# Chaining the chunk products of a state-space scan in TensorE's queue, in six of eight groups

## The chip, the cores and the metric

The kernel runs on one core of one Trainium2 chip. The metric is device time in microseconds of one execution. Three executions of the kernel before were timed, and one more was run under the hardware profiler.

## What is computed

One layer of a hybrid sequence model on a 1024 x 1024 input: a normalised and modulated input `u` goes through one wide projection `w_in`, which feeds a short convolution branch and a Mamba-2 scan; both are projected back, merged by gates, projected by `w_o`, and followed by a squared-ReLU MLP and a last normalisation. The change lies in the scan, which the reference writes so:

```
def step(state, inp):
    xq, aq, bq, cq = inp
    a_cum = jnp.cumsum(aq, axis=1)
    ...
    scores = jnp.einsum('btgn,bsgn->btsg', cq, bq)
    y_diag = jnp.einsum('btsg,btsgr,bsgrp->btgrp', scores, decay, xq)
    y_off = jnp.einsum('btgn,bgrpn->btgrp', cq, state) * jnp.exp(a_cum)[..., None]
    ...
    new_state = (state * jnp.exp(a_cum[:, -1])[..., None, None]
                 + jnp.einsum('bsgn,bsgr,bsgrp->bgrpn', bq, to_end, xq))
    return new_state, y_diag + y_off
```

There are 32 heads in 8 groups; the four heads of a group share `b` and `c`. The kernel cuts the 1024 positions into 8 chunks of 128, which gives the same result as the reference's 16 chunks of 64. All values are float32.

## The kernel before

**Stages.** The projections of the gates, of `z` and of the short convolution come first and last to about 634 us. From there to about 1240 us the scan runs, one group after another (`ssd_group`, L772), and beside it the projections that feed the later groups (`proj_group`, L746). After it come the branch projections (`wco`, L908, begins beside groups 5 to 7; `wso`, from L937), the output projection and the MLP, to 2102 us.

**One chunk of one group** needs five kinds of products on TensorE. The text uses these names for them:

- the *scores* (L779 to L782): the product of `b` and `c` and three transposes, into the PSUM tile `A`, of which there are two;
- the *inner outputs* (L802): four small products of the masked and decayed scores `seg` with `xd`, into the first half of the one PSUM tile `B`;
- the *state outputs* (L807): two products of `c` with the running state, into the second half of `B`; chunk 0 has none;
- the *state update* (L824): one product of `bt` and `xe`, into the one PSUM tile `C`; chunk 7 has none;
- and, once in each group from the second on, the *row sums* of the group before (`finish`, L847; L858 and L859, two pairs), which use the same PSUM tile `C`, after the state update of chunk 4 and before that of chunk 5.

Between them VectorE makes `smk`, `xd`, `xe` out of the scores, multiplies `seg` by `smk`, adds the two outputs (`t1`, L814 and L815), writes them into `xs` (L821, which frees `B`), and forms the next state (L830, L831). ScalarE makes the exponentials out of `acb`, which a transfer on SP's queue brings (L777), and copies `bt`. The tiles of the pool `p2` exist twice.

**The projections beside it.** `proj_group(g + 1)` is traced after the scan of group `g`. It makes four tiles (`xbc_tile`, L732): two of `xs`, one of `bf`, one of `cf`; each is 48 matmuls of 128 x 512 (L121, L122 and L124, 16 each), then two copies by ScalarE into one of two `raw` buffers, a four-tap convolution (ScalarE, three VectorE operations of 1024 columns into one of two `cacc` buffers), and an activation whose result goes to `xs`, `bf` or `cf` of the pool `p2g[g % 2]`. Group `g + 2` writes the same buffers as group `g`, so that this last step waits until the scan of group `g` has read them for the last time.

**What sets the order.** Nobody writes the order of the queues here. A planner in the framework orders each engine's instructions when the kernel is built, by modelled times; what is queued on an engine is then fixed. `tc.issue_after(ins)` adds edges for that planner: what the block traces on the engine of `ins` stands behind `ins` in that engine's queue. It is an edge of order alone; nothing waits for `ins` to end. The kernel before uses it in this stage for the row sums only (L857: behind the state update of chunk 4, which `last` holds).

Of the kernel before, what the change touches and what calls it, by code (L numbers as in the profile page):

```python
# [16 lines left out]
P = 128  # L17
# [21 lines left out]
def hybrid_trunk(tc, xT, par, hrows, crow, wada1, wadak, wada2, win, wdt, wco, wso, wo, wup, wdt_, wdn, out):  # L39
    nc = tc.nc  # L40
    pe, act, dve, pool, sp = nc.tensor, nc.scalar, nc.vector, nc.gpsimd, nc.sync

    def tt(o, a, b, op, eng=dve):
        return eng.tensor_tensor(out=o, in0=a, in1=b, op=op)  # L44

    def stt(o, a, s, b, op0, op1):
        return dve.scalar_tensor_tensor(out=o, in0=a, scalar=s, in1=b, op0=op0, op1=op1)  # L47
# [13 lines left out]
    ident = cp.tile([P, P], F32, name="ident")  # L61
# [471 lines left out]
    for k in range(4):  # L533
# [3 lines left out]
        for i, t in enumerate(ts4):  # L537
            o = [tks[-1].tile([P, H], F32R, name=f"t{i}{j}") for j in (0, 1)]
# [233 lines left out]
    def ssd_group(g, xs, bf, cf, prev):  # L772
        state = None
        for c in range(NC_):
            cs = slice(c * P, c * P + P)
            acb = p2.tile([P, 4, P], F32, name="acb")
            sp.dma_start(acb, ac_d[4 * g:4 * g + 4, cs].partition_broadcast(P))  # L777
            A = psA.tile([P, 512], F32, name="A")
            pe.matmul(A[:, 0:P], lhsT=bf[:, cs], rhs=cf[:, cs], start=True, stop=True)  # L779
            pe.transpose(A[:, 128:256], xs[:, 0, cs], ident)  # L780
            pe.transpose(A[:, 256:384], xs[:, 1, cs], ident)
            pe.transpose(A[:, 384:512], bf[:, cs], ident)  # L782
            smk = p2.tile([P, P], F32, name="smk")
            tt(smk, A[:, 0:P], tri, ALU.mult)
            xd = p2.tile([P, 4, 64], F32, name="xd")
            xq = A[:, 128:384].rearrange("p (r k) -> p r k", r=4)
            tt(xd, xq, dt_t[:, c, 4 * g:4 * g + 4].unsqueeze(2).broadcast_to([P, 4, 64]), ALU.mult)
            if c < NC_ - 1:
                bt = p2.tile([P, P], F32, name="bt")
                act.copy(bt, A[:, 384:512])  # L790
                xe = p2.tile([P, 4, 64], F32, name="xe")
                tt(xe, xq, de_t[:, c, 4 * g:4 * g + 4].unsqueeze(2).broadcast_to([P, 4, 64]), ALU.mult)
            seg = p2.tile([P, 4, P], F32, name="seg")
            for r in range(4):
                hd = 4 * g + r
                act.activation(seg[:, r, :], acb[:, r, :], AF.Relu, bias=acum[:, c, hd:hd + 1], scale=-1.0)
            act.activation(seg, seg, AF.Exp, scale=-1.0)
            tt(seg, seg, smk.unsqueeze(1).broadcast_to([P, 4, P]), ALU.mult)
            Bk = psB.tile([P, 512], F32, name="B")
            for r in range(4):  # L800
                o = 64 * (r % 2)
                pe.matmul(Bk[o:o + 64, P * (r // 2):P * (r // 2) + P], lhsT=xd[:, r, :], rhs=seg[:, r, :],  # L802
                          start=True, stop=True, skip_group_check=True)
            ydv = Bk[:, 0:256].rearrange("p (q t) -> p q t", q=2)
            if c > 0:
                for q in (0, 1):
                    pe.matmul(Bk[:, 256 + P * q:256 + P * q + P],  # L807
                              lhsT=state[:, 2 * q:2 * q + 2, :].rearrange("p r k -> p (r k)"),
                              rhs=cf[:, cs], start=True, stop=True, skip_group_check=True)
                ebc = p2.tile([P, 2, P], F32, name="ebc")  # L810
                for q in (0, 1):
                    act.activation(ebc[64 * q:64 * q + 64], acb[64 * q:64 * q + 64, q::2, :], AF.Exp)
                t1 = p2.tile([P, 2, P], F32, name="t1")
                tt(t1, Bk[:, 256:512].rearrange("p (q t) -> p q t", q=2), ebc, ALU.mult)  # L814
                tt(t1, ydv, t1, ALU.add)  # L815
                src = t1
            else:
                src = ydv
            for q in (0, 1):
                col = DSK + 2 * g + q  # L820
                stt(xs[:, q, cs], xs[:, q, cs], prm[:, col:col + 1], src[:, q, :], ALU.mult, ALU.add)  # L821
            if c < NC_ - 1:
                C = psC.tile([P, H], F32, name="C")[:, 0:256]
                last = pe.matmul(C, lhsT=bt, rhs=xe.rearrange("p r k -> p (r k)"), start=True, stop=True)  # L824
                ns = p2.tile([P, 4, 64], F32, name="state")
                cv = C.rearrange("p (r k) -> p r k", r=4)
                if c == 0:
                    dve.tensor_copy(ns, cv)
                else:
                    tt(ns, state, edec[:, c, 4 * g:4 * g + 4].unsqueeze(2).broadcast_to([P, 4, 64]), ALU.mult)  # L830
                    tt(ns, cv, ns, ALU.add)  # L831
                state = ns
            if c == 4 and prev is not None:
                finish(prev, last)
            if c == 5:
                zs = [p2.tile([P, T], F32, name="zs") for _ in (0, 1)]
                for q in (0, 1):
                    sp.dma_start(zs[q], z_d[2 * g + q])
            if c == 6 and g in (5, 7):
                rstd(*{5: (0, 4), 7: (4, 6)}[g])  # L840
            yield
        for q in (0, 1):
            tt(zs[q], xs[:, q, :], zs[q], ALU.mult)
            pool.dma_start(y_d[2 * g + q], zs[q])
        return g, zs

    def finish(prev, last):  # L847
        g, zs = prev
        for q in (0, 1):
            act.activation(zs[q], zs[q], AF.Square)  # L850
        tt(zs[0], zs[0], zs[1], ALU.add)
        for h in (0, 1):
            sqh, sql = [p2.tile([P, H], F32R, name=n, bufs=1) for n in ("sqh", "sql")]
            split(sqh, sql, zs[0][:, hs[h]])
            row = p2.tile([1, H], F32, name="row", bufs=1)
            ps = psC.tile([P, H], F32, name="C")
            with tc.issue_after(last.ins):  # L857
                pe.matmul(ps, lhsT=onec, rhs=sqh, start=True, stop=False)  # L858
                pe.matmul(ps, lhsT=onec, rhs=sql, start=False, stop=True)  # L859
            act.copy(row, ps[0:1, :])  # L860
            act.dma_start(ssq_d[g:g + 1, hs[h]], row)

    def rstd(g0, g1):
        n = 8 * (g1 - g0)
        sq = p2.tile([32, P], F32, name="sq", bufs=1)[:n]
        sp.dma_start(sq, ssq_d[g0:g1].rearrange("g (c t) -> (g c) t", t=P))
        r = rsqrt_eps(p2, sq, 1.0 / 1024.0, [n, P], "y")
        tsc(r, r, 0.5, None, ALU.mult, ALU.bypass)
        act.dma_start(rst_d[g0:g1].rearrange("g (c t) -> (g c) t", t=P), r)
# [10 lines left out]
    for g in range(NG - 1):  # L880
        gen = ssd_group(g, *cur, prev)
        prev = None
        while prev is None:
            prev = drive(gen)
        cur = proj_group(g + 1)
# [14 lines left out]
    p2t.release()  # L900
    gp = tc.alloc_tile_pool(name="gp", bufs=3, side="right", reuse_waits="tile")
    gen = ssd_group(NG - 1, *cur, prev)
    prev = None
    for f in range(8):
# [107 lines left out]
    for h in (0, 1):  # L1012
        for i in range(4):
            ps, = proj(ws[i], u2h, u2l, halves=(h,))
            r = p6.tile([P, H], F32, name="hid0", bufs=3)
# [6 lines left out]
    for k in range(4):  # L1022
        for i, t in enumerate(tops_of(x1[k] + x1[k + 4], mcol[:, 28 + k:29 + k], dcs[:, k:k + 1])):
            o = [(sl.tile([P, H], F32R, name="s1") if i == 3 else tp.tile([P, H], F32R, name=f"t{i}{k}{j}")) for j in (0, 1)]
# [87 lines left out]
    for s in range(3):  # L1112
# [26 lines left out]
        for n, blk in enumerate((0, 2, 5, 4, 3, 1, 6)):  # L1139
            t = operand([lambda q=q: stage(op_d[s, 2 * q:2 * q + 2, :, blk, :].rearrange("k p t -> p k t")) for q in (0, 1)])  # L1140
            first = n in (0, 2, 3, 5)
            for q in (0, 1):
# [10 lines left out]
                for i in (0, 1):  # L1153
                    p = 2 * q + i
                    if first:
                        bank[p] = mm.tile([P, H], F32, name="mm")
                    o = bank[p]
                    for k in range(4):
                        c_ = slice(i * H + k * P, i * H + k * P + P)
                        for j, (l_, r_) in enumerate(((wh, 0), (wh, 1), (wl, 0))):  # L1160
                            pe.matmul(o, lhsT=l_[:, c_], rhs=t[:, r_, k, :], start=first and k == j == 0,  # L1161
                                      stop=k == 3 and j == 2, skip_group_check=True)
# [13 lines left out]
    for t0, tw, onpool in PARTS:  # L1176
        h, o = t0 // H, t0 % H
# [90 lines left out]
```

## Time and profile before

| | us |
|---|---|
| median of three timed executions | 2101.52 (2098.99 to 2104.03) |
| the profiled execution | 2104.39 |
| its span, first to last instruction | 2102.6 |
| TensorE busy in the span | 2067.2 |
| VectorE busy | 1491.5 |
| ScalarE busy | 962.1 |
| 680 to 1010 us (scan of groups 0 to 4): TensorE, VectorE, ScalarE busy, of 330 | 330.0, 248.2, 224.4 |

A matmul's recorded time overlaps that of the next one, so that TensorE can be "busy" throughout and still lose a tenth of a microsecond between two starts; for that the text goes by the distance of the starts. The mean TensorE clock of the execution was 0.993 of full speed.

### The profile page before, as it was taken

The page shows a single profiled execution, that of the slowest core. Times are in us where ns is not written, and L with a number is a line of the kernel's source. Part 1 is how long each engine was busy: PE and PEld are TensorE (multiplying, and loading weights), DVE is VectorE, ACT ScalarE, POOL GpSimd, SP SyncE. Part 2 cuts the span into 40 slices and gives each one's busy share as a digit, 9 for nine tenths or more (in the row PEclk, how much of TensorE's full clock was granted, in tenths as well). Part 3 has the DMA queues.
Part 4 walks back from the last instruction along what each step waited for, and adds up shares of the span by engine and source line. Part 5 has one row for each costly group of instructions (what it writes and reads, how often), then busy time and mean ns, then how long its engine had stood idle before and what let it go on. Part 6 is the DMA issues. An engine that isn't in the chain of part 4 may idle for free.

```text
span 2102.6 us, 26286 instructions
## 1 busy us (share of the span) xinstructions
PE 2067.2 (98%) x9736; PEld 1693.4 (81%) x9736; DVE 1491.5 (71%) x2348; ACT 962.1 (46%) x1570; POOL 178.2 (8%) x247
## 2 busy tenths in 40 slices
PE   8999999999999999999999999999999999999997
PEld 6878878888887878887788787888888888888887
DVE  8777876776863777777977867936866665658675
ACT  4433333333335676666754541334544454544432
POOL 0010000000001000000000000012000001232213
PEclk8999999999999999999999999999999999999998
DMA  9345543222228454555365779643144447998932
GB/s 326 107 160 184 184 166 121 96 74 71 81 83 252 108 144 128 145 130 127 117 204 205 258 266 338 230 142 115 60 165 165 157 163 261 302 241 253 277 78 81
DMA packets 142578, 355.65 MB, mean 169 GB/s; under 512 B 13505, under 2 KB 48705, under 8 KB 140914
## 3 DMA queue, kind: packets, MB, share of 16 engines
q1 hardware_dynamic: 100002, 206.43, 30.2%
q0 software_dynamic: 27280, 105.39, 17.4%
q10 hardware_dynamic: 15168, 42.15, 5.1%
q8 instruction: 77, 1.26, 0.2%
q14 instruction: 51, 0.42, 0.1%
HBM read 275.08 MB, written 78.84 MB: 168 GB/s over the span
## 4 chain that ended last, share of the span: by engine, by line
PE 75%; issue 14%; DMA 6%; DVE 3%; ACT 1%; POOL 1%; SPq 0%; DVEq 0%; POOLq 0%; ACTq 0%
PE mm L155 30%; PE mm L1161 9%; PE mm L121 9%; PE mm L124 9%; PE mm L122 9%; PE mm L402 2%; PE B L802 1%; PE B L807 1%; DMA wraw<-in_win 1%; DMA wv<-in_wada 1%; DMA dr<-in_wdt_ 1%; PE C L824 1%; POOL wv L550 1%; DMA acb<-ac_d 1%; PE st L402 1%
## 5 line engine op out<-in xcount | busy, mean ns | idle before, releaser
L155 PE MATMUL mm<-t,whi 128*128 128x512 f32 x1168 | 359.3, 389 | 3.8 <-DVE cq L44 3.8
L155 PEld LDWEIGHTS mm<-t,whi 128*128 128x128 f32 x1168 | 218.8, 188 | 50.8 <-DVE cq L44 5.7
L155 PE MATMUL mm<-t,wlo 128*128 128x512 f32 x584 | 226.6, 389 | 0.0
L1161 PE MATMUL mm<-op,whi 128*128 128x512 f32 x672 | 207.1, 389 | 1.2 <-DVE y L47 0.7
L121 PE MATMUL mm<-uh,whi 128*128 128x512 f32 x448 | 177.7, 397 | 1.4 <-ACT raw L738 1.4
L122 PE MATMUL mm<-ul,whi 128*128 128x512 f32 x448 | 177.4, 396 | 0.0
L44 DVE TENSOR_TENSOR wlo<-s,whi 128x1024 fp32r<-128x1024 f32 (+1 forms) x128 | 129.0, 1019 | 67.4 <-ACT whi L160 66.5
L44 DVE TENSOR_TENSOR wlo<-wraw,whi 128x1024 fp32r<-128x1024 f32 (+1 forms) x136 | 144.8, 1065 | 11.7 <-ACT whi L160 5.4
L121 PE MATMUL mm<-ys,whi 128*128 128x512 f32 x384 | 149.3, 393 | 1.5 <-DVE s L44 1.5
L122 PE MATMUL mm<-ys,whi 128*128 128x512 f32 x384 | 150.0, 392 | 0.0
L1161 PEld LDWEIGHTS mm<-op,whi 128*128 128x128 f32 x672 | 126.0, 188 | 28.2 <-ACT whi L1147 2.0
L124 PE MATMUL mm<-uh,wlo 128*128 128x512 f32 x448 | 142.8, 395 | 0.0
L160 ACT CAST whi<-wraw 128x1024 fp32r<-128x1024 f32 x80 | 66.9, 837 | 161.5 <-PE mm L155 143.4
L155 PE MATMUL mm<-s,whi 128*128 128x512 f32 x448 | 138.0, 389 | 0.7 <-ACT cu L178 0.7
L1161 PE MATMUL mm<-op,wlo 128*128 128x512 f32 x336 | 130.7, 389 | 0.0
L160 ACT CAST whi<-s 128x1024 fp32r<-128x1024 f32 x80 | 84.1, 1052 | 99.2 <-PE mm L155 93.1
L155 PEld LDWEIGHTS mm<-t,wlo 128*128 128x128 f32 x584 | 109.6, 188 | 22.9
L124 PE MATMUL mm<-ys,wlo 128*128 128x512 f32 x384 | 125.8, 392 | 0.0
L155 PE MATMUL mm<-uh,whi 128*128 128x512 f32 x312 | 122.4, 392 | 2.4 <-ACT cu L178 2.4
L47 DVE SCALAR_TENSOR_TENSOR y<-mm,mcol,y 128x512 f32<-128x512 f32 (+1 forms) x100 | 69.3, 704 | 76.1 <-PE mm L1161 40.2
L47 DVE SCALAR_TENSOR_TENSOR cacc<-raw,hw,cacc 128x1024 f32<-128x1024 f32 x84 | 107.1, 1278 | 21.3 <-ACT cacc L740 21.0
L155 PE MATMUL mm<-ul,whi 128*128 128x512 f32 x312 | 121.9, 391 | 0.0
(318 smaller groups left out, 4483.0 us busy)
## 6 DMA issues: line engine op xcount, KB each, us to landing
wraw<-in_win SPq DMA_DIRECT2D x83, 512.0 KB, 3.9
dr<-in_wdt_ SPq DMA_DIRECT2D x108, 256.0 KB, 5.2
op_d<-hp POOLq DMA_DIRECT2D x12, 1792.0 KB, 7.1
hr<-op_d POOLq DMA_DIRECT2D x42, 512.0 KB, 6.0
wv<-in_wada POOLq DMA_DIRECT2D x32, 512.0 KB, 4.3
acb<-ac_d SPq DMA_DIRECT2D x64, 256.0 KB, 6.1
wraw<-in_wup SPq DMA_DIRECT2D x32, 512.0 KB, 4.0
wlo<-in_win POOLq DMA_DIRECT2D x28, 512.0 KB, 7.7
```

The lines of the kernel that those rows point to most:

```text
L44: return eng.tensor_tensor(out=o, in0=a, in1=b, op=op)
L47: return dve.scalar_tensor_tensor(out=o, in0=a, scalar=s, in1=b, op0=op0, op1=op1)
L121: pe.matmul(o, lhsT=wh, rhs=h_, start=start, stop=False)
L122: pe.matmul(o, lhsT=wh, rhs=l_, start=False, stop=False)
L124: last_mm[0] = pe.matmul(o, lhsT=wl, rhs=h_, start=False, stop=stop)
L155: last_mm[0] = pe.matmul(o, lhsT=l_[:, s_], rhs=r_, start=first and k == j == 0, stop=k == 3 and j == 2, skip_group_check=True)
L160: act.copy(hi, src)
L402: pe.matmul(sps[f, h], lhsT=w_[f][:, j * P:j * P + P], rhs=v_[j][h], start=j == i == 0, stop=j == KT - 1 and i == 2, skip_group_check=True)
L550: pool.dma_start(w_, wada2[i])
L802: pe.matmul(Bk[o:o + 64, P * (r // 2):P * (r // 2) + P], lhsT=xd[:, r, :], rhs=seg[:, r, :], start=True, stop=True, skip_group_check=True)
L807: pe.matmul(Bk[:, 256 + P * q:256 + P * q + P], lhsT=state[:, 2 * q:2 * q + 2, :].rearrange("p r k -> p (r k)"), rhs=cf[:, cs], start=True ...
L1161: pe.matmul(o, lhsT=l_[:, c_], rhs=t[:, r_, k, :], start=first and k == j == 0, stop=k == 3 and j == 2, skip_group_check=True)
```

## The change

Two blocks are put behind `last`, and `last` is now set by more products. In groups 0 to 5, the state update of a chunk stands behind the last output product of that chunk (the state outputs, or the inner outputs in chunk 0); the scores of chunks 1 to 7 stand behind the state update of the chunk before. The scores of chunk 0, and all of groups 6 and 7, stay free. No arithmetic, no buffer and no transfer is changed. In the call of `finish`, `last` is still the state update of chunk 4.

```
@@ ssd_group @@
             A = psA.tile([P, 512], F32, name="A")
-            pe.matmul(A[:, 0:P], lhsT=bf[:, cs], rhs=cf[:, cs], start=True, stop=True)
-            pe.transpose(A[:, 128:256], xs[:, 0, cs], ident)
-            pe.transpose(A[:, 256:384], xs[:, 1, cs], ident)
-            pe.transpose(A[:, 384:512], bf[:, cs], ident)
+            with tc.issue_after(last.ins) if c and g < 6 else contextlib.nullcontext():
+                pe.matmul(A[:, 0:P], lhsT=bf[:, cs], rhs=cf[:, cs], start=True, stop=True)
+                pe.transpose(A[:, 128:256], xs[:, 0, cs], ident)
+                pe.transpose(A[:, 256:384], xs[:, 1, cs], ident)
+                pe.transpose(A[:, 384:512], bf[:, cs], ident)
...
             for r in range(4):
                 o = 64 * (r % 2)
-                pe.matmul(Bk[o:o + 64, P * (r // 2):P * (r // 2) + P], lhsT=xd[:, r, :], rhs=seg[:, r, :],
-                          start=True, stop=True, skip_group_check=True)
+                last = pe.matmul(Bk[o:o + 64, P * (r // 2):P * (r // 2) + P], lhsT=xd[:, r, :], rhs=seg[:, r, :],
+                                 start=True, stop=True, skip_group_check=True)
...
                 for q in (0, 1):
-                    pe.matmul(Bk[:, 256 + P * q:256 + P * q + P],
-                              lhsT=state[:, 2 * q:2 * q + 2, :].rearrange("p r k -> p (r k)"),
-                              rhs=cf[:, cs], start=True, stop=True, skip_group_check=True)
+                    last = pe.matmul(Bk[:, 256 + P * q:256 + P * q + P],
+                                     lhsT=state[:, 2 * q:2 * q + 2, :].rearrange("p r k -> p (r k)"),
+                                     rhs=cf[:, cs], start=True, stop=True, skip_group_check=True)
...
                 C = psC.tile([P, H], F32, name="C")[:, 0:256]
-                last = pe.matmul(C, lhsT=bt, rhs=xe.rearrange("p r k -> p (r k)"), start=True, stop=True)
+                with tc.issue_after(last.ins) if g < 6 else contextlib.nullcontext():
+                    last = pe.matmul(C, lhsT=bt, rhs=xe.rearrange("p r k -> p (r k)"), start=True, stop=True)
```

## The prediction, made before the change was run

> **What bounds the kernel now.** I read the page first, then the busy time by stretch, then TensorE's waits, and last the order of time on TensorE in the scan.
>
> ```profile
> PE 2067.2 (98%) x9736; PEld 1693.4 (81%) x9736; DVE 1491.5 (71%) x2348; ACT 962.1 (46%) x1570; POOL 178.2 (8%) x247
> ```
>
> ```profile
> 134.00:140.00 6.00, 3.66 (x9) 2.94 (x10) 5.80 (x11) 3.58 (x7) 0.00 (x0) 0.72 0.07 10
> 680.00:1010.00 330.00, 330.00 (x1787) 265.32 (x1786) 248.18 (x484) 224.42 (x454) 24.35 (x32) 1.00 0.52 129
> 1010.00:1210.00 200.00, 196.44 (x1043) 158.41 (x1042) 164.43 (x294) 116.39 (x229) 2.13 (x4) 1.00 0.61 203
> ```
>
> ```profile
> PE C L824 <- DVE xe L44: 2.0, 2, 1.3
> PE mm L121 <- DVE s L44: 1.5, 1, 1.5
> PE mm L121 <- ACT raw L738: 1.4, 1, 1.4
> PE B L802 <- DVE seg L44: 1.1, 1, 1.1
> PE B L802 <- DVE t L44: 0.8, 1, 0.8
> ```
>
> The columns of the second fence are the stretch and its length, the busy time (and count) of TensorE, weight load, VectorE, ScalarE and GpSimd, the granted clock, the share of the DMA engines and GB/s. In the scan of groups 0 to 4 TensorE is never free, at full clock. The third fence holds all its waits from 660 to 1290 us: 6.8 us together. So this stage ends when TensorE's work ends, and that work is the same after the change: nothing is removed. A gain can come only from cheaper switching between the products, or out of those 6.8 us. A loss has no such cap.
>
> **Switching.** The planner already puts many products side by side. One such run on TensorE (start, duration):
>
> ```profile
> 705.00 0.39 PE L121 MATMUL mm<-uh,whi 128*128 128x512 f32 x1
> 705.32 0.66 PE L802 MATMUL B<-seg,xd 128*64 128x128 f32 x8
> 705.91 0.71 PE L807 MATMUL B<-cf,state 128*128 128x128 f32 x4
> 706.46 0.60 PE L824 MATMUL C<-xe,bt 128*128 128x256 f32 x2
> 706.89 0.38 PE L779 MATMUL A<-cf,bf 128*128 128x128 f32 x2
> ...
> 707.36 0.48 PE L122 MATMUL mm<-ul,whi 128*128 128x512 f32 x1
> 707.67 0.40 PE L121 MATMUL mm<-uh,whi 128*128 128x512 f32 x1
> 707.90 0.39 PE L122 MATMUL mm<-ul,whi 128*128 128x512 f32 x1
> ```
>
> ```profile
> 694.34 0.59 PE L824 MATMUL C<-xe,bt 128*128 128x256 f32 x2
> 694.59 0.59 PE L122 MATMUL mm<-ul,whi 128*128 128x512 f32 x1
> 695.01 0.40 PE L121 MATMUL mm<-uh,whi 128*128 128x512 f32 x1
> ```
>
> A projection product takes 0.23 us of the queue (707.67 to 707.90). From the projection product ahead of the run to the second one behind it are 2.67 us; less two products that leaves 2.2 us for all of a chunk's products. Inside, the state update takes 706.46 to 706.89, 0.43 us. Alone between projection products it takes 694.34 to 695.01 less one product, 0.44 us. So leaving the projections and coming back costs 0.01 us. The change can save one or two such switches in 48 chunks: 0 to 1 us. I take 0.5 us.
>
> **What the edges move.** Before, the state update stands one chunk ahead of its outputs, and the scores up to three. The first fence below is the tile `C` from 970 to 992 us (group 4: count, shortest, median and longest in ns, first and last start), the second is TensorE in order of time:
>
> ```profile
> L824 PE MATMUL C<-xe,bt x4: 377/378/483, 971.4 to 991.8; 128*128 128x256 f32 x4
> L858 PEld LDWEIGHTS C<-sqh,onec x2: 186/189/192, 978.3 to 984.7; 128*128 128x128 f32 x2
> L858 PE MATMUL C<-sqh,onec x2: 475/489/503, 978.3 to 984.7; 128*128 128x512 f32 x2
> ```
>
> ```profile
> 674.55 0.66 PE L802 MATMUL B<-seg,xd 128*64 128x128 f32 x8 [1.12 <-DVE seg L44]
> ...
> 977.29 0.66 PE L802 MATMUL B<-seg,xd 128*64 128x128 f32 x8
> 977.87 0.71 PE L807 MATMUL B<-cf,state 128*128 128x128 f32 x4
> ...
> 997.33 0.60 PE L807 MATMUL B<-cf,state 128*128 128x128 f32 x4
> ...
> 1003.23 0.66 PE L802 MATMUL B<-seg,xd 128*64 128x128 f32 x8
> ```
>
> The last inner outputs (1003.23) are those of chunk 7 of group 4, and the first (674.55) of chunk 0 of group 0: 39 chunks apart, 328.7 us, so 8.4 us a chunk. After the change the scores start only behind the chunk before, and the next inner outputs need them through VectorE. Its prices:
>
> ```profile
> L44 DVE TENSOR_TENSOR smk<-A,tri x41: 272/281/293, 682.1 to 1000.4; 128x128 f32<-128x128 f32 x41
> L44 DVE TENSOR_TENSOR xd<-A,dt_t x40: 402/418/425, 682.3 to 1003.9; 128x256 f32<-128x256 f32 x40
> L44 DVE TENSOR_TENSOR seg<-seg,smk x40: 673/682/693, 684.4 to 1008.7; 128x512 f32<-128x512 f32 x40
> ```
>
> ```profile
> L47 DVE SCALAR_TENSOR_TENSOR cacc<-raw,hw,cacc 128x1024 f32<-128x1024 f32 x60 | 76.5, 1277 | 7.6 <-ACT cacc L740 7.5
> ```
>
> ```profile
> 994.73 0.41 DVE L44 TENSOR_TENSOR state<-C,state 128x256 f32<-128x256 f32 x1
> ```
>
> *An ordinary chunk.* The loop is now the run of products (2.2), `smk` 0.28, `xd` 0.42, `seg` 0.68, and one convolution step 1.28 that can lie in between: 4.9 us. In the queue a product stands later than its operand: the state of chunk 6 is there at 995.14 (994.73 + 0.41), the product that reads it starts at 997.33, 2.2 us later, filled with projections. With that lead the loop is 7.1 us, under the 8.4 us that a chunk takes anyway. Without any convolution step it is 5.8; with two, and `xe` ahead of `seg`, 8.8. I take 7.1, so that ordinary chunks cost nothing: the projections cover the loop. No transfer is moved, and SP's loads of `acb` hang on ScalarE's work, which needs no scores. If that cover is gone, the bare 4.9 us lie open, less 2.2 of own work: 2.7 us of idle TensorE a chunk.
>
> *The row sums.* Here I expect the price. The state update of chunk 4 (971.4), two pairs of row sums (978.3, 984.7) and the state update of chunk 5 (last record 991.8) share one PSUM tile and stand some 6.7 us apart. Chunk 6's scores were done long before. After the change the first stands behind the state outputs of chunk 4, at 977.87 + 0.55 instead of 971.4: 7.0 us later; all behind it moves along, and now the scores of chunk 6 too, which stand behind the state update of chunk 5. Queued behind that update on TensorE, if the planner leaves no projections there, is everything else. Bounds: 0 a group, if the row sums close up by as much (their own work is under a microsecond a pair), and 11, if the loop of chunk 6 to 7 grows by another 4. I take 7, what the lead was. Groups 1 to 4: 28 us by which the scan falls back on the projections. (In group 5 the branch projections stand ready as cover.)
>
> **Whether falling back costs time.** TensorE fills it with projections, as far as there are any:
>
> ```profile
> 640.00:674.50 34.50, 17.57 (x45) 8.26 (x44) 1.00 0.94 302
> 674.50:1003.20 328.70, 137.25 (x346) 65.06 (x346) 1.00 0.52 129
> ```
>
> ```profile
> 1008.81 2.01 ACT L743 ACTIVATE xs<-cacc 128x1024 f32<-128x1024 f32 x2 [1.10 <-DVE zs L44]
> ```
>
> These rows count the products of L121, 16 a tile: 391 by 1003.2 us are 24.4 tiles, while groups 1 to 5 use 20. The projections are 4.4 tiles ahead. The next step of a tile waits for the end of the scan (1008.81, released by `zs`); two tiles fit into `cacc`, two into `raw`, two into PSUM: 6. So 1.6 tiles are left, 48 x 0.23 us each: 18 us. Of the 28 us that leaves 10 uncovered. A chunk without cover loses its lead of 2.2 us and shows 2.7 us of idle, so each takes 4.9 out of the 10: two chunks, 5.5 us idle. With 11 a group it is (44 - 18) / 4.9 x 2.7 = 14 us; with 4 or less, nothing.
>
> **Sum.** 2104.4 - 0.5 + 5.5 = 2109.4 for the profiled execution, which lies 2.9 us above the median; for the median 2106.5. The end of that reckoning at 14 us gives 2115; the middle of the two, 2110.8. Because every cover in it (all six places used, the planner finding them) is taken at its best, I forecast 2109.
>
> **Rivals.**
>
> *No change (within 0.2%, 4.2 us, about what a measurement of this kernel tells from none).* The row sums close up, or the six places hold; then 2101 to 2104. For it: not one wait in 330 us, VectorE free for a quarter of it. The change doing nothing is no part of this: the order at 971 and 977 us must turn.
>
> *Faster.* With scores no longer three chunks ahead, VectorE's early work on later chunks no longer stands before `t1` and `xs` of this one, the loop falls below 8.4 us, the scan ends sooner, and projections are left over for groups 6 and 7. That takes the waits behind 1010 us: 6.8 less 1.8 at the start (the 1.1 on `seg` at 674.55 and the smaller of the two on `xe`, 0.7) is 5.0, and 1 us of switching: 2095.5. It decides if a group from 1 to 4 takes less than 8 x 8.4 = 67 us. Against it: the row sums.
>
> *Much slower, by the ordinary loop.* With 8.8 us, and waits in the order that the planner did not foresee, each of 31 chunks adds 0.4 to 1 us; with 28 from the row sums that is 40 to 59, less 18, over 4.9, times 2.7: 12 to 23 us, so 2113 to 2124. And the clock can fall. In the stretch from 134 to 140 us TensorE was free for 2.3 of 6 us and the clock 0.72; if each of 4 to 8 gaps costs 0.28 of 6 us, 1.7 us, that adds 7 to 14, up to 2138. [...]
>
> **How the numbers follow.** Forecast (slower by 0.2 to 0.6%): 0.34. Much slower: 0.15. No change: 0.32, since the forecast's lower end runs into it. Faster: 0.19. As the forecast is one side of two close cases, its own range is 2105 to 2115. The range over all reaches from the faster rival's end at 2095 to 2130, which leaves out some 0.1 of clock losses above and 0.07 below.
>
> **What would show it.** Right: on TensorE, L807, L824 and L779 stand in this order in every chunk of groups 0 to 5; the state update of chunk 5 comes some 7 us later behind the inner outputs of chunk 4 than the 14 us of before; waits of L802 on `seg` appear towards the ends of groups 2 to 4, 2 to 3 us each. Wrong: groups of 67 us or less, or L802 waiting in ordinary chunks from group 0 on, which would put the price into the loop; or new waits only behind 1210 us, where no step of this looks.

## The result and the profile after

The changed kernel takes 2178.72 us (median of four, 2175.91 to 2179.91), beside 2100.26 us for the kernel before (four, 2098.86 to 2104.03). The ratio is 1.0375, with a 95% interval of 1.0359 to 1.0391: 78 us slower, where the prediction had 2109.0 and 2130 as its upper end. The profiled execution took 2178.78 us, 74.4 more than that of before. Lines of the file have moved on by one or two: inner outputs L803, state outputs L808, state update L826, scores L780 to L783, row sums L860 and L861.

The page's row of busy times, and the waits of TensorE from 640 to 1400 us (sum, times, longest):

```profile
PE 2084.6 (96%) x9736; PEld 1707.6 (78%) x9736; DVE 1491.9 (69%) x2348; ACT 966.3 (44%) x1570; POOL 178.8 (8%) x247
```

```profile
PE B L803 <- DVE seg L44: 30.5, 7, 9.1
PE mm L121 <- ACT raw L738: 20.5, 2, 10.7
PE C L860 <- DVE state L44: 3.6, 1, 3.6
```

The same work is done, but these three waits alone are 54.6 us, where all of TensorE's waits had been 6.8. The two large ones belong together, as the next two views show. First the busy time by stretch, columns as in the prediction:

```profile
640.00:825.50 185.50, 182.59 (x948) 148.30 (x946) 103.09 (x192) 108.70 (x209) 12.31 (x15) 1.00 0.57 148
825.50:848.40 22.90, 11.85 (x66) 8.99 (x65) 20.29 (x36) 18.23 (x37) 1.97 (x3) 0.67 0.51 152
848.40:903.60 55.20, 55.19 (x277) 44.78 (x277) 29.67 (x63) 27.68 (x56) 2.63 (x3) 0.98 0.39 91
903.60:925.80 22.20, 7.31 (x47) 5.42 (x46) 17.52 (x30) 16.54 (x32) 2.00 (x3) 0.68 0.46 131
```

Then the products of L121 (16 a projection tile) by stretch: length, TensorE and weight load with counts, clock, DMA:

```profile
640.00:825.50 185.50, 84.49 (x215) 40.40 (x215) 1.00 0.57 148
825.50:848.40 22.90, 0.00 (x0) 0.00 (x0) 0.67 0.51 152
848.40:903.60 55.20, 25.50 (x64) 12.28 (x64) 0.98 0.39 91
925.80:983.70 57.90, 25.96 (x64) 12.41 (x64) 0.97 0.41 96
1006.80:1065.00 58.20, 26.09 (x64) 12.53 (x64) 0.97 0.34 86
```

Read them together. Up to 825 us next to nothing is lost: TensorE is busy for 182.59 of 185.50 us, at full clock. The first of these products starts at 633.35 us and 9 of them stand ahead of 640, so that by then (215 + 9) / 16 = 14.0 tiles are made. The scan is at the last chunk of group 1, and groups 1 and 2 take 8: the projections are 6.0 tiles ahead of it. Then comes a stretch of 23 us without one projection product, a *hole*. Exactly 64 products later, four tiles, comes the next one, and so on, four times (824.9 to 848.4, 903.1 to 925.8, 983.1 to 1006.8, 1064.6 to 1091.0). I take as *lost* in a hole its length, from the start of the row with the last two projection products to that of the next, less these two (0.5 us) and the scan's own products in it at full clock. In the third that is 23.6 - 5.2 - 0.5 = 17.9 us; the four lost 15.6, 17.0, 17.9 and 18.5, 69 us in all. By the same count over all starts from 640 to 1320 us, some 90 us are lost after the change and some 17 before. The difference is all but a few of the 74.4 us by which the profiled executions differ.

**Why the projections come so far ahead.** An ordinary chunk (chunk 3 to 4 of group 3), TensorE and then VectorE in order of time:

```profile
944.14 0.66 PE L803 MATMUL B<-seg,xd 128*64 128x128 f32 x8
944.73 0.71 PE L808 MATMUL B<-cf,state 128*128 128x128 f32 x4
945.28 0.60 PE L826 MATMUL C<-xe,bt 128*128 128x256 f32 x2
945.71 0.38 PE L780 MATMUL A<-cf,bf 128*128 128x128 f32 x2
...
946.73 0.39 PE L121 MATMUL mm<-uh,whi 128*128 128x512 f32 x1
...
952.85 0.39 PE L122 MATMUL mm<-ul,whi 128*128 128x512 f32 x1
953.17 0.66 PE L803 MATMUL B<-seg,xd 128*64 128x128 f32 x8
```

```profile
946.92 0.28 DVE L44 TENSOR_TENSOR smk<-A,tri 128x128 f32<-128x128 f32 x1
...
947.97 0.68 DVE L44 TENSOR_TENSOR seg<-seg,smk 128x512 f32<-128x512 f32 x1
948.58 0.42 DVE L44 TENSOR_TENSOR xe<-A,de_t 128x256 f32<-128x256 f32 x1
954.50 0.42 DVE L44 TENSOR_TENSOR t<-B,ebc 128x256 f32<-128x256 f32 x1 [5.51 <-PE B L808]
```

The order is the one that the change asks for. From the inner outputs to the `seg` of the next chunk it takes 948.65 - 944.14 = 4.5 us. But the product that reads it stands another 4.5 us further back in the queue, behind projections, and VectorE has nothing to do for 5.5 us. The chunk takes 9.0 us. No wait shows, since TensorE is full (busy for 9.03 of these 9.03 us, at clock 1.00); the queue's order alone holds the scan back. Group 0 (first inner outputs to those of group 1) went from 62.0 us to 78.6 (672.66 to 751.29), without any row sums in it.

**What a hole is.** The third one in order of time, over all engines:

```profile
983.15 0.61 PE L124 MATMUL mm<-uh,wlo 128*128 128x512 f32 x2
983.69 0.66 PE L803 MATMUL B<-seg,xd 128*64 128x128 f32 x8
...
986.48 2.35 DVE L44 TENSOR_TENSOR zs<-xs,zs 128x1024 f32<-128x1024 f32 x2
...
988.97 1.99 ACT L743 ACTIVATE xs<-cacc 128x1024 f32<-128x1024 f32 x2
...
991.07 2.35 DVE L47 SCALAR_TENSOR_TENSOR xs<-xs,cacc 128x1024 f32<-128x1024 f32 x2
991.29 1.12 PE L803 MATMUL B<-seg,xd 128*64 128x128 f32 x8 [3.40 <-DVE seg L44]
...
996.02 1.06 ACT L852 ACTIVATE zs<-zs 128x1024 f32<-128x1024 f32 x1 [4.39 <-DMA y_d<-zs]
996.98 1.23 ACT L740 ACTIVATE cacc<-raw,hb,hw 128x1024 f32<-128x1024 f32 x1
998.12 1.26 ACT L797 ACTIVATE seg<-acb,acum 128x128 f32<-128x128 f32 x4
998.24 1.28 DVE L47 SCALAR_TENSOR_TENSOR cacc<-raw,hw,cacc 128x1024 f32<-128x1024 f32 x1 [4.16 <-ACT cacc L740]
...
1002.70 2.46 DVE L47 SCALAR_TENSOR_TENSOR cacc<-raw,hw,cacc 128x1024 f32<-128x1024 f32 x2
...
1005.20 1.06 ACT L743 ACTIVATE bf<-cacc 128x1024 f32<-128x1024 f32 x1 [2.07 <-DVE cacc L47]
1006.16 1.05 ACT L738 COPY raw<-mm 128x512 f32<-128x512 f32 x2
1006.78 0.79 PE L121 MATMUL mm<-uh,whi 128*128 128x512 f32 x1 [10.69 <-ACT raw L738]
```

The last two projection products (983.15) fill the last place. Then the group's last outputs, `zs`, the activations into the freed `xs`, the next `cacc`, its convolution, the copy that frees PSUM, and only then the next projection product. All of it goes through the queues of ScalarE and VectorE, and the scan of the next group stands in the same queues: on ScalarE, `cacc` (996.98) and then the `seg` of the scan (998.12) come behind the square that waited 4.39 us.

### The profile page after: what moved, and what is told of

It reads as the page before. It is cut to its first block, busy times and chain, and to the rows that moved or that the text cites. A ratio compares the mean times of both kernels' runs of the same rounds, so it can differ in the third digit from the quotient of the medians.

```text
span 2177.0 us, 26313 instructions
## 1 busy us (share of the span) xinstructions
PE 2084.6 (96%) x9736; PEld 1707.6 (78%) x9736; DVE 1491.9 (69%) x2348; ACT 966.3 (44%) x1570; POOL 178.8 (8%) x247
## 4 chain that ended last, share of the span: by engine, by line
PE 70%; issue 15%; DMA 8%; DVE 5%; ACT 1%; POOL 1%; SPq 0%; DVEq 0%; POOLq 0%; ACTq 0%
PE mm L155 29%; PE mm L1163 9%; PE mm L121 8%; PE mm L122 8%; PE mm L124 8%; PE mm L402 2%; DMA y_d<-zs 1%; DMA dr<-in_wdt_ 1%; DMA wraw<-in_win 1%; PE st L402 1%; PE B L808 1%; DMA yr<-y_d 1%; PE B L803 1%; PE sx L402 1%; DMA wv<-in_wada 1%
## 5 line engine op out<-in xcount | busy, mean ns | idle before, releaser
L121 PE MATMUL mm<-uh,whi 128*128 128x512 f32 x448 | 178.7, 399 | 20.6 <-ACT raw L738 20.5
L122 PE MATMUL mm<-ul,whi 128*128 128x512 f32 x448 | 177.5, 396 | 0.0
L121 PE MATMUL mm<-ys,whi 128*128 128x512 f32 x384 | 149.7, 392 | 3.0 <-ACT gt L953 3.0
L124 PE MATMUL mm<-uh,wlo 128*128 128x512 f32 x448 | 145.9, 396 | 0.0
L797 ACT ACTIVATE seg<-acb,acum 128x128 f32<-128x128 f32 x256 | 81.9, 390 | 93.3 <-PE B L803 79.9
L155 PE MATMUL mm<-uh,wlo 128*128 128x512 f32 x312 | 121.9, 391 | 0.0
```

The source lines that it names most:

```text
L121: pe.matmul(o, lhsT=wh, rhs=h_, start=start, stop=False)
L122: pe.matmul(o, lhsT=wh, rhs=l_, start=False, stop=False)
L124: last_mm[0] = pe.matmul(o, lhsT=wl, rhs=h_, start=False, stop=stop)
L155: last_mm[0] = pe.matmul(o, lhsT=l_[:, s_], rhs=r_, start=first and k == j == 0, stop=k == 3 and j == 2, skip_group_check=True)
```

## The experiments

Theory at this point: the ties make the scan slower than the projections; nothing is lost until the places for tiles are full, and from then on every group ends in a hole. What slows the scan was open. The first expectations put it on the row sums between tied updates and named the loop through the scores as rival B. The other rivals: the row sums alone as the whole price (the prediction's step), the lower clock, or the order in the queue itself. Each comparison is with runs of the kernel before on the same chip (2098.1 to 2101.6 us). Tiles are counted here from the first product of L121, which starts between 629 and 637 us; the expectations count from 640 us, which gives 0.3 to 0.9 less.

**Each tie alone.** First the state update alone:

```
-            with tc.issue_after(last.ins) if c and g < 6 else contextlib.nullcontext():
+            with contextlib.nullcontext():
                 pe.matmul(A[:, 0:P], lhsT=bf[:, cs], rhs=cf[:, cs], start=True, stop=True)
```

> Only the state update is put behind its chunk's outputs; the scores stay free. Theory (the ties slow the scan against the projections beside it; nothing is lost until the projections have filled the six places ahead of the scan, and then each group's end shows a hole of some 23 us without projections, 17 us of it lost): row sums move by 7 us a group, scores do not, so a group takes 75 us instead of 68 and the lead grows by 1.1 tiles a group; the six places are full at the end of group 4 only: 2100 to 2120 us, one hole or none. Rival A (the row sums' chain alone is the whole price): most of the 78 us, 2160 to 2180. Rival B (the ordinary loop through the scores is the price): 2098 to 2104.

2111.45 us, ratio 1.0051 (1.0035 to 1.0066); one large hole, 950.0 to 970.8 us, at 22 tiles. Group 0 takes 60.5 us (62.0 before), so that the tie costs an ordinary chunk nothing, but groups 1 to 3, with row sums in them, take 72.8, 74.8 and 74.1, where they took 67.1, 70.6 and 66.0 before. The other way round, with the same edit at the state update:

> Only the scores are put behind the state update of the chunk before; the state update stays free. Theory: the scores keep one chunk of lead, only those of chunk 6 wait for the row sums; 2100 to 2120 us, with one hole at most. Rival A (row sums alone): like the other half-change, 2100 to 2180, whichever half carries it. Rival B (ordinary loop): nearly all of the price, 2150 to 2180, and waits of the inner outputs on seg in ordinary chunks.

2155.33 us, 1.0262 (1.0191 to 1.0333); group 0 takes 81.3 us, and holes come at 14, 18, 22 and 26 tiles. The theory on record missed (2100 to 2120): the time is that of rival B, and the scores' tie makes most of the loss. The waits in ordinary chunks that rival B had named are not there (TensorE waits 3.2 us in all from 640 to 830 us), so the loop acts through the pace alone. From here on the theory has both, the loop and the row sums.

**A looser tie of the scores.** They stand behind the state update of two chunks back; all else as in the change.

```
+        upd = []
-            with tc.issue_after(last.ins) if c and g < 6 else contextlib.nullcontext():
+            with tc.issue_after(upd[-2]) if c > 1 and g < 6 else contextlib.nullcontext():
...
+                upd.append(last.ins)
```

> Both ties stay, the row sums stay at chunk 4, but the scores of a chunk stand behind the state update of the chunk before the last one, not of the last one. Theory (the loop through the scores is what slows the scan): the loop of 9.0 to 12.7 us may now go round once in two chunks, 16.8 us, so the scores' tie costs nothing and the kernel is that with the state update tied alone, 2111: 2106 to 2118, one large hole without projections, near 21 tiles. Rival (any tie of the scores costs, by what the planner does with the other engines): four holes again, 2145 to 2180.

2112.76 us, 1.005 (1.0033 to 1.0067), which is the kernel with the update tied alone. Group 0 takes 60.9 us. There were two holes of 14 and 15 us instead of one large one. So it is the loop within one chunk that costs, not a tie of the scores as such.

**The row sums elsewhere.** `finish`, and the load of `zs`, go to chunk 6:

```
-            if c == 4 and prev is not None:
+            if c == 6 and prev is not None:
                 finish(prev, last)
-            if c == 5:
+            if c == 6:
                 zs = [p2.tile([P, T], F32, name="zs") for _ in (0, 1)]
```

With both ties:

> Both ties as in the change, but the row sums of the group before are traced after the state update of chunk 6 instead of chunk 4 (the load of z moves with them), so that they stand between no two updates of one group. Theory: half of the delay goes (the next group's first update still waits for them), the lead grows more slowly, and two or so of the four holes go: 2130 to 2160 us. Rival A: 2100 to 2110. Rival B: 2175 to 2180, no change.

2141.3 us, 1.0195 (1.0114 to 1.0277): 37 us better than the changed kernel. There are still four holes, but two of them are of 8 and 9 us. With the state update tied alone, and, as a control, without any tie:

> Only the state update tied, and the row sums traced behind the state update of chunk 6. Theory: without the row sums between two tied updates the scan keeps the pace of before, the six places never fill, no hole: 2096 to 2104 us. If the state update's tie slows ordinary chunks by itself: 2105 to 2112, with a hole.

> The kernel before, with only the row sums moved behind chunk 6, as a control for the two runs that use this place. Theory: TensorE is full in both, 2097 to 2103 us; more than that would mean that the new place has a price of its own.

2088.15 us, 0.9952 (0.9935 to 0.9969), and 2089.24, 0.9958 (0.9942 to 0.9974). Both are faster than the kernel before, and lie below what I had expected of either. The products of L121 in that first one, one row a group (1 to 4):

```profile
719.80:781.80 62.00, 26.23 (x66) 12.42 (x66) 1.00 0.56 138
781.80:843.40 61.60, 25.42 (x64) 12.04 (x64) 1.00 0.56 137
843.40:904.90 61.50, 25.42 (x64) 12.04 (x64) 1.00 0.54 137
904.90:966.50 61.60, 25.42 (x64) 12.04 (x64) 1.00 0.55 137
```

Four tiles a group, in just the time that TensorE needs for them (192 x 0.227 + 8 x 2.2 = 61.2 us): here the scan keeps pace, and at the last chunk of each of groups 0 to 4 the lead is some 2.5 tiles. In the kernel before, groups 1 to 4 took 66 to 71 us, and this lead grew from 2.5 to 4.8. Some 8 us are lost from 640 to 1320 us, in the control too, where it was some 17. So the row sums behind chunk 4 had cost some 9 us before the change; the state update's tie is free once they are out of its way. With the looser scores' tie as well:

> As the last, and the row sums at chunk 6. Theory: the projections' lead over the scan stays at about 1.8 tiles in all groups, no hole, 2085 to 2095, as with the state update tied alone and the sums at chunk 6 (2088). Rival (the row sums' move helps only a scan whose scores are free): lead over 4 tiles, at least one hole, above 2100.

2093.2 us, 0.9954 (0.9937 to 0.9971), as expected, but not with the steady lead of the expectation: groups 2 to 4 took 67 to 70 us, and the lead at the last chunk grew to 5.9 tiles in group 5, which still fits into six places. Of these three none is shown better than another.

**Ties in two groups only** (`g < 6` becomes `g < 2` in both blocks):

> Both ties, in groups 0 and 1 only. Theory: the places are full at the end of group 1, one hole of 17 to 18 us there; the free groups 2 to 4 still gain half a tile each on the scan, so smaller holes of some 5 us at their ends: 2118 to 2140 us. Rivals A and B (a price a tied group, paid where it is tied): two sixths of 78 us, 2126, with waits spread over groups 0 and 1 and none later.

2125.34 us, 1.0119 (1.0051 to 1.0187). The time fits the rivals too (2126); the place of the loss does not. The hole at 14 tiles is there in full (822.0 to 850.5 us, 16.9 lost), and of the groups behind it, which are untied, two still show holes, of 7.6 and 12.1 us. So the loss is not a price paid where a group is tied: it depends on the lead that is left.

**More places.** A third `cacc` buffer, and then a fourth, for which the branch buffer `ccs` has to go from three to two:

```
-        a = p2t.tile([P, T], F32, name="cacc")
+        a = p2t.tile([P, T], F32, name="cacc", bufs=3)
```

> Both ties as in the change, with a third cacc buffer, so that the projections have one more place ahead of the scan. Theory: the first hole comes when the projections have reached 18.5 tiles and not 13.5, so that the hole at the end of group 1 is gone, and the later ones come one tile later (18.5, 22.5, 26.5); three holes of 17 us at most: 2150 to 2165 us. Rivals (the tie costs by its own loop in TensorE's queue, or by the row sums, whatever room there is): 2175 to 2180.

> As the run before with four cacc buffers, for which the later stage's ccs goes from three buffers to two: two more places. Theory: holes at about 19.5, 23.5 tiles or later, two of them: 2130 to 2150 us. Rivals: 2175 to 2180.

With three: 2152.0 us, 1.0254 (1.0221 to 1.0287). L121 in it, up to the first hole and then by group:

```profile
640.00:903.30 263.30, 113.62 (x290) 54.34 (x290) 0.99 0.54 139
903.30:978.00 74.70, 25.32 (x64) 12.32 (x64) 0.91 0.43 111
978.00:1054.90 76.90, 25.55 (x64) 12.41 (x64) 0.90 0.34 92
```

With the 14 products ahead of 640 us, the first hole comes at (290 + 14) / 16 = 19 tiles, one group later and one tile further, and there are three of 19 to 27 us instead of four. With four `cacc` they begin where they should, at 20, 24 and 28 tiles, but these are three and not two, and the time is 2169.83, 1.0339 (1.0313 to 1.0364), not the 2130 to 2150 expected: a new hole of 48 us (25.8 lost) stands behind the last projection. Its control is the kernel before with these buffers:

> The kernel before, without ties, with four cacc buffers and two of the buffers that load the convolution branch (ccs) instead of three. It tells where the 48 us hole behind the last projections came from in the tied kernel with the same buffers. Theory (the missing ccs buffer makes it): a hole of over 10 us behind the last projection here too, 2108 to 2130. Rival (the ties make it, since with more places the projections are used up while three groups of the scan are still to come): no such hole, 2096 to 2104.

2116.75 us, 1.0076 (1.0047 to 1.0105), with such a hole too (1075.4 to 1098.2, 13.8 lost). By these two figures about half of the new loss is the missing `ccs` buffer's.

**Fewer places, and no tie at all:**

```
-    padded = [p2t.tile([P, T + 32], F32, name=f"raw{i}", bufs=1) for i in (0, 1)]
+    padded = [p2t.tile([P, T + 32], F32, name=f"raw{i}", bufs=1) for i in (0,)]
...
-        a = p2t.tile([P, T], F32, name="cacc")
+        a = p2t.tile([P, T], F32, name="cacc", bufs=1)
```

> The kernel before, without ties, with one raw and one cacc buffer instead of two each: four places for projections ahead of the scan instead of six. Theory (only the places decide, and the ties act through the lead alone): in the kernel before the projections are 3.5, 3.9 and 4.5 tiles ahead when groups 3, 4 and 5 begin; a limit near 3.6 is reached at the end of group 2 or 3, so one to three holes of 10 to 25 us from 15.6 or 19.6 tiles on, 2110 to 2145. Rival (the holes need the ties' order in the queue): no hole over 5 us, 2098 to 2108.

2122.22 us, 1.0103 (1.0069 to 1.0136). L121 by group (2 to 4), and the end of a hole in group 4:

```profile
797.70:862.90 65.20, 25.30 (x64) 12.03 (x64) 1.00 0.52 131
862.90:928.10 65.20, 25.32 (x64) 12.04 (x64) 1.00 0.52 129
928.10:994.60 66.50, 25.51 (x65) 12.22 (x65) 1.00 0.53 127
```

```profile
942.87 0.46 PE L779 MATMUL A<-cf,bf 128*128 128x128 f32 x2 [2.93 <-DVE xe L44]
```

The lock at four tiles a group comes from the places alone: the holes begin at 12, 16, 20 and 24 tiles, four ahead of the scan each time, and there are four places. These holes, of 5 to 7 us, each with 1.7 to 3.4 lost, and one of 15.5 at the end, are smaller than expected.

**What sets a hole's length.** I had put it down to the convolution of the parked tiles. This leaves out two of its four taps:

```
-        for j in (2, 1, 0):
+        for j in (0,):
             stt(a, raw[:, j:j + T], hw[:, 4 * ci + j:4 * ci + j + 1], a, ALU.mult, ALU.add)
```

> Both ties as in the changed kernel, but the convolution leaves out two of its four taps: one VectorE step of 1.28 us a tile instead of three. Theory (the hole is the refill chain of the parked tiles): the holes begin where they began, with the projections 5.6 tiles ahead, and each is shorter by two steps of each of two parked tiles, 4 x 1.28 = 5 us, so 17 to 19 us instead of 23; with four holes 2150 to 2165. Rival (the hole is the scan's own loop at the lower clock, beside which the convolution runs for nothing): holes of 22 us and more, 2168 to 2182.

> The control: the kernel before, without ties, with the same two taps left out. Nothing there waits for the convolution except the few waits between 1010 and 1290 us, so both theories have 2094 to 2102; below 2090 the taps would cost time of their own, and the run with ties has to be read against this one.

2148.08 us, 1.0252 (1.0221 to 1.0283), and the control 2094.34, 0.9968 (0.9953 to 0.9982). The time is just below what the theory had, but the holes are not as it had them: the first shrank to 8.1 us, since the scan fell back less before it, and the other three were 21.2, 22.4 and 19.9 us, 1.5, 1.2 and 6.5 shorter than in the changed kernel. Next in the chain is the square of `zs` on ScalarE, which waits 4.39 us for the transfer to `y_d` (row at 996.02), with `cacc` queued behind it. Here the squares get a tile of their own:

```
+            zq = p2.tile([P, 2, H], F32, name="zq", bufs=1)
+            for q in (0, 1):
+                act.activation(zq[:, q, :], zs[q][:, hs[h]], AF.Square)
+            tt(zq[:, 0, :], zq[:, 0, :], zq[:, 1, :], ALU.add)
```

> The control: the kernel before, the squares of the row sums written to a tile of their own instead of over zs, so that ScalarE needn't wait for the transfer of zs to y_d. There is no hole for the wait to lengthen: 2094 to 2103 by both theories.

> Both ties, and the squares in a tile of their own. Theory (a hole is a chain of steps in the in-order queues of ScalarE and VectorE, the square's wait for the transfer among them): in holes 2 to 4 the cacc behind the square starts 2.7, 3.6 and 1.8 us earlier, and the second cacc no longer stands behind a second square: 8 to 14 us less than 2179, 2164 to 2171. Rival (the wait is beside another that ends as late): 2174 to 2182.

> Both ties, the squares apart, and one convolution step of three as in the run with two taps left out (2148). Theory: both parts of the chain are shorter, and the two gains add up: another 8 to 14 us, 2134 to 2141, holes of 16 to 19 us. Rival (the scan's own loop at the lower clock takes over as the last to end): 2143 to 2152.

Without ties 2108.73 us, 1.0026 (1.0012 to 1.004), slower than either theory had it, with a new hole of 10 us behind 1022.8, which makes it a poor control; with ties 2172.02, 1.0337 (1.0305 to 1.0369), between the two ranges; with one convolution step 2151.24, 1.0236 (1.0207 to 1.0266), where the rival had it. ScalarE's waits in the hole, 980 to 1010 us, of the second of these:

```profile
ACT seg L797 <- PE B L803: 5.5, 1, 5.5
ACT seg L797 <- DMA acb<-ac_d: 4.5, 1, 4.5
```

The wait for `y_d` is gone, and just ahead of `cacc` in ScalarE's queue stands one of 4.5 us for `acb` instead; the four holes are 20 to 29 us. A hole has several steps that end nearly together, so that taking one away brings little. Which of them would have to go together to close it stays open.

## Why the prediction was wrong

**The step that failed: "With that lead the loop is 7.1 us, under the 8.4 us that a chunk takes anyway. ... I take 7.1, so that ordinary chunks cost nothing."** The loop proper was right (4.9 with a convolution step; 4.5 measured without). The lead was not: 2.2 us, read from one row of the kernel before, where after the change it is 4.5 us. 4.5 + 4.5 is 9.0, over 8.4, and with two or three convolution steps in them chunks of group 0 took 9.0 to 12.0. Group 0 alone fell back by 16.6 us, where the step had nothing. The sign that I had named for this case, waits of this product (now L803) in ordinary chunks from group 0 on, did not show, for the price lies in the queue's order and not in a wait. The length of a group, which I had named as a sign for the faster rival alone, showed it at once. The scores' tie alone and the looser tie show that this loop is the cause. Why the planner leaves 4.5 us there was not tested.

**Second, the price of an uncovered stretch.** "A chunk without cover loses its lead of 2.2 us and shows 2.7 us of idle, so each takes 4.9 out of the 10: two chunks, 5.5 us idle." Measured are 15.6 to 18.5 us lost a group, with about three chunks in the hole. The step reckoned with a scan that goes on by its bare loop. But when the places are full, ScalarE and VectorE must first work off the parked tiles, and the scan waits in their queues (`seg` is late by up to 9.1 us). Which step of this chain ends last was not settled.

**Right or nearly so.** *The places:* "two tiles fit into `cacc`, two into `raw`, two into PSUM: 6"; the projections stopped at 6.0, and they stop at 7 with one place more, at 8 with two more and at 4 with two fewer. How many were left was misread: the rows from 640 us leave out the 7 products ahead of it. From the first one (635.64) to 1003.2 us there are 397, 24.8 tiles, so that the lead was 4.8 tiles and not 4.4, and the cover left 13 us and not 18. By the prediction's own sum that makes 8 us idle instead of 5.5, far from the 74. *The row sums:* 7 us a group with bounds of 0 and 11. With the state update alone tied, groups 1 to 3 take 73.9 us on average, where they took 67.9 before: 6.0 us. That kernel, 12 us slower, is about what the prediction described. Its detail was off: behind the inner outputs of chunk 4 (953.17) the state update of chunk 5 came at 970.29, 17.1 us later, not 14 + 7. *Switching* brings nothing to speak of: in the chunk above, the products between two projection products (943.82 to 946.73, less three of 0.227) take 2.2 us, as before. *Rivals:* "much slower, by the ordinary loop" had the mechanism, but at 0.4 to 1 us a chunk, where group 0 shows 16.6 / 8 = 2.1, and with the wrong price of a stretch without cover, so it ended at 2138.

**The clock.** It was at half speed from 833.16 to 850.23 us, from 911.66 to 928.73, from 990.17 to 1010.65 and from 1072.09 to 1092.57, one stretch for each hole. TensorE was busy in them for 10.47, 6.64, 8.44 and 10.02 us. A product of 512 columns started 0.43 us after the one before there (1007.37 and 1007.80), and not 0.23. If half of this busy time was due to the clock, and all of it lay on the path, the clock in the holes cost at most 17.8 us of the 78. That it ends last anywhere was not shown; it was not tried by itself.

## What to carry to other kernels

An edge in a queue can slow a stage without a wait that shows it (group 0 took 78.6 us instead of 62.0, and TensorE waited 3.0 us in all from 640 to 825 us), so measure the pace of the tied stage (start to start over a group) against that of the work that fills its gaps. Here the difference cost next to nothing until the six places between the two were full, at 825 us, and from then on it was paid in every round, 15.6 to 18.5 us a group, together with the work that had piled up in the other engines' queues; read it from the lead in tiles, not from idle time. A step that sits inside a chain, like the row sums here, is worth moving out of it first: that gained 9 us even without a tie.

## What the runs showed of the hardware

The idle time ahead of a lower TensorE clock was not one number. The kernel before at 136 us:

```profile
132.91 1.08 PE L572 MATMUL st<-sel,dtT 64*128 64x32 f32 x8
136.34 0.80 PE L155 MATMUL mm<-uh,whi 128*128 128x512 f32 x1 [2.35 <-ACT cu L178]
136.94 0.63 PE L155 MATMUL mm<-ul,whi 128*128 128x512 f32 x1
```

After 2.35 us idle a product of 512 columns takes 0.63 us instead of 0.39. After 3.40 us idle in the hole above the four inner outputs take 1.12 instead of 0.66. But after 2.93 us idle without ties (row at 942.87) the transposes that follow take their usual 0.27 us. The first two places by stretch, TensorE alone (length, busy time and count, clock, DMA): the kernel before, then the changed kernel:

```profile
132.84:136.25 3.41, 1.15 (x9) 1.00 0.22 90
136.25:139.66 3.41, 3.32 (x8) 0.50 0.11 14
```

```profile
986.76:990.17 3.41, 1.13 (x7) 1.00 0.81 184
990.17:1010.65 20.48, 8.44 (x28) 0.50 0.45 134
```

In both, TensorE was busy for 1.15 or 1.13 us of the 3.41 us ahead of the lower clock, which then lasted 3.41 and 20.48 us. The changed kernel, at about the place of the first, shows the same fall with much more work ahead of it:

```profile
133.43:136.84 3.41, 2.46 (x15) 1.00 0.00 0
136.84:140.25 3.41, 3.41 (x10) 0.50 0.43 137
```

The one wait in the first of these rows is 0.95 us. From 640 to 1320 us the kernel before was at clock 1.00 throughout. The changed kernel was at 0.50 in six stretches: the four of the holes (17.07, 17.07, 20.48 and 20.48 us) and two of 3.41 us, from 1266.65 and from 1280.30 us. What decides when the clock falls was not shown.
